# Prompt attention of a hybrid decoder layer: all heads' keys ahead of the values, four heads' scores in one row of small matmuls, four heads' outputs in another

## The chip, the cores and the metric

One core of one Trainium2 chip runs one launch of the whole layer. The metric is the device time of that launch in microseconds (us).

## The reference, cut to what matters

One layer of a decoder for a prompt (256 positions) and 8 samples of 4 positions, 288 columns in all, in float32. The change is in the prompt's half of "mixer B", an attention with three head groups of four heads; head `j` of the three groups is merged into one output with softmax weights over all three groups' keys together:

```python
z = jnp.einsum('ntd,de->nte', x, w_in)
h, gate_b, gate_c, q, k, v, g_a, g_b = jnp.split(z, _split_points(), axis=-1)
ya, conv_mix_new = _causal_dwconv(gate_c * h, conv_mix_prev, w_conv_mix)
ya = gate_b * ya
...
for g, (win, dil) in enumerate(GROUPS):          # (128,1), (512,4), (2048,16)
    o, l = _dilated_band_prompt(q[:, :, g], kg, vg, slopes[g], dil)
wg = jax.nn.softmax(jnp.stack(lses), axis=0)
yb = jnp.einsum('gnth,gnthd->nthd', wg, jnp.stack(outs)).reshape(n, t, ATT_OUT).astype(x.dtype)
mixed = jax.nn.sigmoid(g_a) * (ya @ w_branch_a) + jax.nn.sigmoid(g_b) * (yb @ w_branch_b)
x1 = _layernorm(ALPHA * x + mixed @ w_out, ln1_g, ln1_b)
```

Then a convolutional feed-forward (`w_up`, `w_down`) and a second layer norm. `yb` is needed only by the product with `w_branch_b`.

## The kernel before, in words

**Products.** TensorE (PE) multiplies 128 output features at a time. One block of weights (128 x 2048 values, 1 MB) is loaded by SP into one of three buffers `wst`, and split into a high and a low part: ACT casts `whi` (line 260), DVE subtracts `wlo` (line 260), each in two halves of the block, into four half-block buffers each. `product` (line 234) takes a block that is ready, has the next one prepared, and issues 48 matmuls (`mms`, lines 254 to 256: 16 slices of the contraction, three terms each) into one of five PSUM tiles `acc`. These five tiles are handed out in turn. A half-block's buffer comes free when PE has passed the half-block four halves earlier, so ACT's cast waits for PE, and all that stands behind the cast on ACT waits with it. The engines run their instructions in order; a scheduler sets the order when the program is built, and `behind` and `in_a_row` add edges to it.

**Order of the products.** Three query blocks (`first_three`), nine more, then for each head `j` six products: the keys and values of the three groups by turns (lines 857 to 883), then 16 triples for the short convolution (h, gate c, gate b; lines 928 to 945), the gates and the two branch products, `w_out`, the feed-forward.

**The prompt's attention** is driven by a generator, `prompt`, that `prompt_step` (line 225) advances after each product by the number that it yielded. Its pieces are:
- *Scores*: `score_row` (line 471) issues 24 small matmuls for a head (32 output columns each, line 490) behind the last matmul of a product, in one unbroken row on PE.
- *Softmax*: `softmax` (line 506): DVE adds distances (line 512), maximum (519), scale (520), ACT exponentiates (521), DVE normalises (522, 523).
- *Turning*: `weights` and `values` transpose 32 x 32 squares on DVE (line 455, helper `squares`), and `moved` puts each of 16 squares of a tile in its place: the 4 on the diagonal on POOL (line 459) at once, the other 12 as copies on ACT (463) or DVE (461), queued in `soon` and issued a few per product.
- *Outputs*: `output_row` (line 430) issues 48 small matmuls for a head (line 443) into one `acc` tile; ACT and DVE then split it into `ybh`, `ybl` (line 260), two pieces a head on each.

There are three rows of small matmuls. The first holds the scores of heads 0 to 2, behind head 2's last product. The second holds the scores of head 3 and the outputs of heads 0 to 2, behind head 3's last product. The third (`last_output`, line 704) holds head 3's output; it is issued some 27 products later from the list of the samples' steps.

**The samples' attention** runs beside it as another generator, `steps`, one step a product (paused for `N_PAUSE` = 5 products after the first score row). In a step half a tile of cached keys is multiplied, by POOL (line 613, one `tensor_tensor` of 128 x 1024) or ACT (line 611, eight activations), and DVE folds it (line 619).

**Buffers.** Keys and values of two heads stand in `kv`; the turned weights and values of heads 0 to 2 in `p_three`, `v_three`, those of head 3 in `late_p`, `late_v`.

Of the kernel before, what the change touches and what calls it, by code (L numbers as in the profile page):

```python
# [10 lines left out]
F32 = mybir.dt.float32  # L11
# [6 lines left out]
P = 128  # L18
D = 2048
KD = D // P  # L20
SEQ = 256
# [88 lines left out]
def layer_kernel(ctx: ExitStack, tc: tile.TileContext, ins, outs):  # L110
# [63 lines left out]
    def weight_list():  # L174
        for b in range(3, NB_QKV + 3 * KD):
            yield ins["w_in"][b], KD
# [176 lines left out]
    def pa_take(n):  # L353
        pa_at[0] += n
        return pa[:, pa_at[0] - n : pa_at[0]]


    m_near = [pa_take((1 + h) * P) for h in range(2)]
    m_all = [pa_take((NG - 1) * (1 + h) * P).rearrange("p (g k) -> p g k", g=NG - 1) for h in range(2)]
    k_third = [m_all[1].rearrange("p g k -> p (g k)")[:, g * SEQ : (g + 1) * SEQ] for g in range(NG - 1)]  # L360
    k_first = pa_take(SEQ)
# [9 lines left out]
    sT, s_squares = (xs_flat[:, n + c * MB * P : n + (c + 1) * MB * P].rearrange("p (b q) -> p b q", q=P) for c in range(2))  # L371


    def in_q(at, n):
        return xs_flat[:, at : at + n * P].rearrange("p (b k) -> p b k", k=P)

    p_three = sT, in_q(0, MB), in_q(MB * P, MB)
    v_three = (*v_two, in_q(2 * MB * P, 2 + NC))
# [44 lines left out]
    o_next = []  # L423
# [6 lines left out]
    def output_row():  # L430

        row = []
        quadrants = [slice(a, a + 32) for a in range(0, P, 32)]
        for j, v, p in o_next:
# [15 lines left out]
        o_next.clear()  # L450
        return row
# [19 lines left out]
    def score_row(heads):  # L471
# [5 lines left out]
        for n, (j, kT, k_class) in enumerate(heads):  # L477
            second = sb(ps, [P, 512], *(("att", F32, 2), ("long", F32, 1), ("acc",))[n])
            near_at = second[:, 3 * P :] if n == 2 else first[:, n * w : n * w + P]
            far_at = first[:, n * w : (n + 1) * w - P] if n == 2 else first[:, n * w + P : (n + 1) * w]  # L480
# [13 lines left out]
        if o_next:  # L494
            some_moves(len(soon))
            row += output_row()
# [42 lines left out]
    def early_head(j, vT):  # L539
        values(vT)  # L540
        moved(v_three[j], v_squares)
        yield 1

    def three_heads(heads, vT):

        no_keys()
        s3 = score_row(heads)
        pause[0] = N_PAUSE
        n_moves[0] = N_MOVES_TWO
        for n, j in enumerate((2, 0, 1)):  # L550
            softmax(j, s3[j])
            yield 1
            weights(p_three[j])
            no_keys()
            if n == 0:
                values(vT)
                moved(v_three[2], v_squares, True)
            yield 1
        o_next.extend(zip(range(3), v_three, p_three))

    def last_head(head, vT):

        s3 = score_row([head])
        softmax(head[0], s3[0])
        values(vT)
        moved(late_v, v_squares)
        yield 1
        weights(late_p)
        yield 2
        o_next.append((head[0], late_v, late_p))  # L570
# [3 lines left out]
    kv = dd_all[:, : 2 * 2 * NG * T].rearrange("p (b c g t) -> p b c g t", b=2, c=2, g=NG)  # L574
    sw = [dd_all[:, 2 * 2 * NG * T :], sb(wk, [P, (NB + 1) * NH * NS], "sw", bufs=1)]

    late_p, late_v = (
        dd_all[:, a * P : b * P].rearrange("p (b k) -> p b k", k=P) for a, b in ((0, MB), (MB, MB + 2 + NC))
    )
# [59 lines left out]
    def sample_steps():  # L639
# [64 lines left out]
        def last_output():  # L704
            some_moves(len(soon))
            all_heads[0] = True
            row = output_row()
            in_a_row([last_mm[0]] + row)

# [90 lines left out]
        for which, order in (("ck", far + near), ("cv", near + far)):  # L800
# [8 lines left out]
            if which == "ck":  # L809
                at(when + 2, key_spread, 1)  # L810
                at(when + 2, key_spread, 0)
                for d, what in ((3, key_sum), (3, last_output), (5, scores)):
                    at(when + d, what)
# [44 lines left out]
    for j in range(NH):  # L858
        kT, vT = (kv[:, j % 2, c] for c in range(2))
        k_class = []  # L860
        for g in range(NG):
            for t in (kT, vT):
                o = product(x).rearrange("p h a -> p a h")
                act.copy(t[:, g, :].rearrange("p (a h) -> p a h", h=2), o)
                if j == g == 0 and t is kT:
                    act.copy(k_first.rearrange("p (a h) -> p a h", h=2), o[:, :P])
                if g and t is kT:
                    if j == 2:
                        k = k_third[g - 1]
                    else:  # L870
                        k = sb(wk, [P, YW], "cy", bufs=2) if j else sb(wk, [P, UW + 2], "u", bufs=2)
                    k_class.append(k[:, :SEQ].rearrange("p (c i) -> p c i", c=NC))
                    act.copy(k_class[-1], o.rearrange("p a h -> p (a h)")[:, :SEQ].rearrange("p (i c) -> p c i", c=NC))
        pool.tensor_copy(k_s[:, :, j, :], kT[:, :, SEQ:])
        pool.tensor_copy(v_s[:, j], vT[:, :, SEQ:])
        act.dma_start(outs["o_k"][j].rearrange("p (g t) -> p g t", g=NG), kT)
        act.dma_start(outs["o_v"][j].rearrange("p (g t) -> p g t", g=NG), vT)
        heads.append((j, k_first if j == 0 else kT[:, 0], k_class))
        if j < 2:
            prompt[:] = [early_head(j, vT), 0]  # L880
        else:
            prompt[:] = [three_heads(heads[:3], vT) if j == 2 else last_head(heads[3], vT), 0]
        prompt_step()
# [605 lines left out]
```

## Time and profile before

| | |
|---|---|
| median of 3 runs | 1703.39 us (1703.29 to 1703.5) |
| profiled execution | 1703.31 us, its span 1701.1 us |
| PE busy | 1694.8 us (100%) |
| DVE, ACT, POOL busy | 1207.7 (71%), 945.5 (56%), 400.0 us (24%) |
| the three rows of small matmuls begin at | 182.33, 220.95 and 384.33 us |

The span is the time from the first to the last instruction of one profiled execution; that execution took 2.21 us more in all. In a timeline each row gives start, duration, engine, line, operation, what it writes and reads, how many instructions are merged, and in brackets how long the engine stood idle before it and what ended that. Matmuls overlap, so the distance between starts says more of PE than a duration does.

### The profile page before, as it was taken

The numbers are of one execution on the slowest core, as the hardware profiler recorded it, in microseconds if no ns is written. First come the engines' busy times: TensorE is split into PE (matmuls) and PEld (weight loads), VectorE is DVE, ScalarE is ACT, GpSimd is POOL, SyncE is SP. The second block draws the span as 40 slices with busy tenths as digits, with TensorE's granted clock in tenths as the row PEclk, the third lists the DMA queues.
The fourth block names the chain that finished last, engine by engine and source line by source line (L and its number), as shares of the span: only waits on it lengthen the run. The fifth ranks groups of instructions, "written<-read, shape, count | busy, mean of one in ns | idle before, by whom it ended". The sixth has DMA issues, their size and how long they took to land.

```text
span 1701.1 us, 34294 instructions
## 1 busy us (share of the span) xinstructions
PE 1694.8 (100%) x14086; PEld 1690.4 (99%) x14086; DVE 1207.7 (71%) x1574; ACT 945.5 (56%) x1696; POOL 400.0 (24%) x530
## 2 busy tenths in 40 slices
PE   9999999999999999999999999999999999999998
PEld 9999999999999999999999999999999999999998
DVE  5476779889887777655888888855686554555575
ACT  5577686665666655544556565544455443344454
POOL 0122243223332221110464233300111100011165
PEclk9999999999999999999999999999999999999999
DMA  8788778666678888677766666666666666666663
GB/s 293 294 300 348 283 283 317 239 253 243 249 297 314 332 306 337 210 259 257 284 230 223 225 252 235 230 223 226 235 228 252 224 233 236 249 224 230 226 241 137
DMA packets 59805, 436.17 MB, mean 256 GB/s; under 512 B 7744, under 2 KB 12608, under 8 KB 19904
## 3 DMA queue, kind: packets, MB, share of 16 engines
q1 hardware_dynamic: 58352, 430.15, 68.7%
q10 hardware_dynamic: 1296, 3.83, 0.6%
q8 instruction: 110, 1.80, 0.4%
q14 instruction: 47, 0.39, 0.1%
HBM read 427.50 MB, written 94.53 MB: 307 GB/s over the span
## 4 chain that ended last, share of the span: by engine, by line
PE 99%; POOL 0%; ACT 0%; POOLq 0%; issue 0%; ACTq 0%
PE acc L254 32%; PE acc L255 32%; PE acc L256 32%; PE acc L339 1%; POOL sw L1145 0%; PE acc L443 0%; PE acc L270 0%; PE att L490 0%; PE acc L490 0%; POOLq L1484 0%; PE long L490 0%; ACT yah L1187 0%; PE att L1043 0%; ACT cache L1103 0%; PE att L1039 0%
## 5 line engine op out<-in xcount | busy, mean ns | idle before, releaser
L260 DVE TENSOR_TENSOR wlo<-wst,whi 128x1024 fp32r<-128x1024 f32 (+1 forms) x578 | 743.8, 1289 | 391.0 <-ACT whi L260 388.3
L260 ACT CAST whi<-wst 128x1024 fp32r<-128x1024 f32 (+1 forms) x578 | 588.9, 1021 | 652.7 <-PE acc L255 593.0
L254 PE MATMUL acc<-xh,whi 128*128 128x288 f32 (+1 forms) x3216 | 920.6, 286 | 0.0
L256 PE MATMUL acc<-xh,wlo 128*128 128x288 f32 (+1 forms) x3216 | 920.4, 286 | 0.0
L255 PE MATMUL acc<-xl,whi 128*128 128x288 f32 (+1 forms) x3216 | 920.3, 286 | 0.0
L254 PEld LDWEIGHTS acc<-xh,whi 128*128 128x128 f32 x3216 | 607.8, 189 | 0.5 <-issue 0.4
L256 PEld LDWEIGHTS acc<-xh,wlo 128*128 128x128 f32 x3216 | 607.8, 189 | 0.0
L255 PEld LDWEIGHTS acc<-xl,whi 128*128 128x128 f32 x3216 | 607.8, 189 | 0.0
L255 PE MATMUL acc<-yal,whi 128*128 128x288 f32 x1216 | 347.7, 286 | 0.0
L256 PE MATMUL acc<-yah,wlo 128*128 128x288 f32 x1216 | 347.7, 286 | 0.0
L254 PE MATMUL acc<-yah,whi 128*128 128x288 f32 x1216 | 347.6, 286 | 0.0
L255 PEld LDWEIGHTS acc<-yal,whi 128*128 128x128 f32 x1216 | 229.8, 189 | 0.0
L256 PEld LDWEIGHTS acc<-yah,wlo 128*128 128x128 f32 x1216 | 229.8, 189 | 0.0
L254 PEld LDWEIGHTS acc<-yah,whi 128*128 128x128 f32 x1216 | 229.8, 189 | 0.0
L909 POOL COPY qk_s<-u 128x2 f32<-128x2 f32 x44 | 36.5, 830 | 532.6 <-ACT u L1247 412.1
L897 DVE SCALAR_TENSOR_TENSOR cy<-u,prm,cy 128x304 f32<-128x304 f32 x120 | 75.8, 632 | 8.1 <-ACT cy L895 4.9
L613 POOL TENSOR_TENSOR cache<-cache,cst 128x1024 f32<-128x1024 f32 x16 | 34.5, 2160 | 110.0 <-DMA cache<-in_cv 94.9
L613 POOL TENSOR_TENSOR cache<-cache,qk_s 128x1024 f32<-128x1024 f32 x16 | 33.9, 2122 | 74.3 <-DMA cache<-in_ck 74.0
L260 ACT CAST yah<-ya 128x288 fp32r<-128x288 f32 x76 | 32.6, 429 | 32.1 <-DVE ya L920 14.5
L611 ACT ACTIVATE cache<-cache,qk_s 128x128 f32<-128x128 f32 x128 | 40.6, 392 | 0.0
L890 POOL COPY u<-prm 128x16 f32<-128x16 f32 x60 | 40.4, 674 | 0.2 <-issue 0.2
L611 ACT ACTIVATE cache<-cache,cst 128x128 f32<-128x128 f32 x128 | 40.0, 390 | 0.0
(277 smaller groups left out, 1181.3 us busy)
## 6 DMA issues: line engine op xcount, KB each, us to landing
wst<-in_w_in SPq DMA_DIRECT2D x112, 1024.0 KB, 5.5
wst<-in_w_up SPq DMA_DIRECT2D x88, 1024.0 KB, 4.9
wst<-in_w_down SPq DMA_DIRECT2D x32, 1024.0 KB, 4.9
cache<-in_ck SPq DMA_DIRECT2D x18, 1024.0 KB, 8.2
cache<-in_cv SPq DMA_DIRECT2D x18, 1024.0 KB, 8.6
wst<-in_w_a SPq DMA_DIRECT2D x16, 1024.0 KB, 6.1
wst<-in_w_out SPq DMA_DIRECT2D x16, 1024.0 KB, 5.0
wst<-in_w_down SPq DMA_DIRECT2D x16, 768.0 KB, 4.5
```

The lines of the kernel that those rows point to most:

```text
L254: pe.matmul(out, hi[:, c, :], xh_k, start=k == 0, stop=False)
L255: pe.matmul(out, hi[:, c, :], xl_k, start=False, stop=False)
L256: last_mm[0] = pe.matmul(out, lo[:, c, :], xh_k, start=False, stop=k == nk - 1)
L260: return act.copy(hi, src), dve.tensor_tensor(lo, src, f32(hi), ALU.subtract)
L339: i = pe.matmul(o[b], first_w(term == 2, b, k), xk, start=k == 0 and term == 0, stop=k == KD - 1 and term == 2,)
L611: behind(act.activation(o[:, a, b], t[:, a, b], AF.Copy, scale=w[:, a, b : b + 1]), w_split[0])
L613: behind(pool.tensor_tensor(o, t, w.unsqueeze(3).broadcast_to([P, *n]), ALU.mult), w_split[1])
L890: pool.tensor_copy(tail[:, :, 0:2], prm[:, state : state + 2 * NB].rearrange("p (b r) -> p b r", b=NB))
L897: dve.scalar_tensor_tensor(y, u[:, i : i + YW], prm[:, w0 + i : w0 + i + 1], y, ALU.mult, ALU.add)
L909: pool.tensor_copy(dst[:, 0:2], u[:, SEQ : SEQ + 2])
```

## The change

The projection's blocks are now taken in another order: all 12 key products of the four heads first, then all 12 value products. Behind the last key product one row holds the scores of all four heads (the fourth head's long scores go to a second `acc` tile). The softmaxes then run beside the value products in the order of heads 2, 3, 0, 1; each head's values are turned when they are there (heads 1 and 2 with the copies on DVE, 0 and 3 on ACT). Behind the second product of the convolution (gate c of the first triple) one row holds the outputs of all four heads. The row out of the samples' steps is gone. The three-row version's number of small matmuls is kept: 96 for scores and 192 for outputs.

```diff
     def weight_list():
-        for b in range(3, NB_QKV + 3 * KD):
-            yield ins["w_in"][b], KD
+        n = NG * NH
+        for blocks in (range(3, n), range(n, NB_QKV, 2), range(n + 1, NB_QKV, 2), range(NB_QKV, NB_QKV + 3 * KD)):
+            for b in blocks:
+                yield ins["w_in"][b], KD
...
     def output_row():
-        row = []
+        row = [last_mm[0]]
...
-        for j, v, p in o_next:
+        for j, (v, p) in enumerate(zip(v_heads, p_heads)):
...
-        o_next.clear()
-        return row
+        in_a_row(row)
...
     def score_row(heads):
-            second = sb(ps, [P, 512], *(("att", F32, 2), ("long", F32, 1), ("acc",))[n])
...
+            second = sb(ps, [P, 512], *(("att", F32, 2), ("long", F32, 1), ("acc",), ("acc",))[n])
...
-        if o_next:
-            some_moves(len(soon))
-            row += output_row()
         in_a_row(row)
         return s3
...
+    def values_of(j, on_dve=False):
+        some_moves(len(soon))
+        values(v_done[j])
+        moved(v_heads[j], v_squares, on_dve)
+
+    def four_heads(heads):
         no_keys()
         s3 = score_row(heads)
         pause[0] = N_PAUSE
         n_moves[0] = N_MOVES_TWO
-        for n, j in enumerate((2, 0, 1)):
+        for n, j in enumerate((2, 3, 0, 1)):
             softmax(j, s3[j])
             yield 1
-            weights(p_three[j])
+            weights(p_heads[j])
             no_keys()
...
+            yield 2 if n == 0 else 1
+            if n:
+                values_of(n - 1, n > 1)
+                yield 1 if n < NH - 1 else 2
+        values_of(NH - 1)
         yield 2
+        some_moves(len(soon))
+        output_row()
...
     for j in range(NH):
...
+            o = product(x).rearrange("p h a -> p a h")
+            act.copy(kv[:, j, g].rearrange("p (a h) -> p a h", h=2), o)
...
+        heads.append((j, kv[:, j, 0], k_class))
+    prompt[:] = [four_heads(heads), 0]
+    prompt_step()
+    for j in range(NH):
+        for g in range(NG):
+            o = product(x).rearrange("p h a -> p a h")
+            act.copy(kv[:, j, g].rearrange("p (a h) -> p a h", h=2), o)
...
+        v_done.append(kv[:, j])
+    prompt_step()
```

The line numbers of the changed program stand some lines off those of before (254 to 256 are 256 to 258 there, 260 is 262, 443 is 446, 455 is 457, 463 is 465, 613 is 604, 619 is 610, 936 is 920).

**PE, at the end of the row that holds the outputs.** A name like `acc_2938` is one handing-out of an `acc` tile. Before, on PE, the end of the second row (the last score matmuls went ahead of it), with what each waits for:

```order
L443 MATMUL acc_2833<-yah_88,yal_178 32x256 [waits Activation_49,Pool_49]
L443 MATMUL acc_2833<-yah_88,yal_178 32x256 x3
L443 MATMUL acc_2833<-yah_88,yal_178 32x2x32 x16
L443 MATMUL acc_2833<-yah_88,yal_178 32x128 x4
L443 MATMUL acc_2862<-yah_88 32x256 x4
L443 MATMUL acc_2862<-yah_88 32x2x32 x16
L443 MATMUL acc_2862<-yah_88 32x128 x4
L254 MATMUL acc_2938<-xh_86,whi_2702 128x288
```

And of the change, the fourth head of the one row of outputs (`acc_3076`) and the first matmul of the product behind it, gate b of the first triple (`acc_3138`):

```order
L446 MATMUL acc_3076<-yah_88,yal_178 32x256 [waits Activation_49,Pool_49]
L446 MATMUL acc_3076<-yah_88,yal_178 32x256 [waits Pool_49] x2
L446 MATMUL acc_3076<-yah_88,yal_178 32x256 [waits Activation_49,Pool_49]
L446 MATMUL acc_3076<-yah_88,yal_178 32x2x32 x16
L446 MATMUL acc_3076<-yah_88,yal_178 32x128 x4
L256 MATMUL acc_3138<-xh_86,whi_2927 128x288 [waits DVE_49,PE_49]
```

What moved: before, the product behind the row waits for no other engine; now its first matmul waits for DVE. With four output tiles in a row, the next product gets the `acc` tile of the product just ahead of the row (`acc_2937`, gate c), and that is read by DVE's line 920.

**ACT, around that row.** Before, on ACT, behind head 3's last value product (`acc_2712`):

```order
L611 ACTIVATE cache_2002<-cache_2002,qk_s_182 128x128 x2
L864 COPY dd_184<-acc_2712 128x288
L611 ACTIVATE cache_2002<-cache_2002,qk_s_182 128x128 x6
L463 COPY dd_184<-yal_178 32x6x32 x6
L877 DMA out_o_v<-dd_184 128x864
L260 CAST ybh_180<-acc_2804 128x128
L260 CAST ybh_180<-acc_2833 128x128
```

Of the change, on ACT: the 12 copies of head 3's turned values (line 465, `yal_178`) stand between the casts of the weights for the products gate b (`whi_2927`, `whi_2931`) and the next triple's h (`whi_3119`); `h_2923` is the product h of the first triple:

```order
L262 CAST whi_2927<-wst_2925 128x1024
L465 COPY yal_178<-yal_178 32x6x32 x9
L262 CAST whi_2931<-wst_2925 128x1024
L465 COPY yal_178<-yal_178 32x6x32 x2
L915 COPY h_2923<-acc_2865 128x288
L465 COPY yal_178<-yal_178 32x6x32
L262 CAST whi_3119<-wst_3116 128x1024
```

What moved: head 3's values used to be turned long after the second row and were needed at the third; now they are the last thing that the row of outputs needs, and a weight cast and the copy of h stand among their copies.

**DVE, up to the read of `acc_2937`.** Before, on DVE, ahead of and behind the second row's start:

```order
L455 STREAM_TRANSPOSE yah_88<-yal_178 128x640
L260 TENSOR_TENSOR wlo_2703<-wst_2700,whi_2702 128x1024
L260 TENSOR_TENSOR wlo_2707<-wst_2700,whi_2706 128x1024
L619 TENSOR_REDUCE dd_184<-cache_1862 128x2x4x4
L455 STREAM_TRANSPOSE yal_178<-dd_184 128x256
L455 STREAM_TRANSPOSE yal_178<-dd_184 128x4x64
L260 TENSOR_TENSOR wlo_2920<-wst_2917,whi_2919 128x1024
```

Of the change, from the copies of head 2's values on DVE (line 463) to gate c's read (line 920):

```order
L463 COPY yah_88<-yal_178 32x6x32 x12
L262 TENSOR_TENSOR wlo_2847<-wst_2844,whi_2846 128x1024
L457 STREAM_TRANSPOSE yal_178<-dd_184 128x4x64
L262 TENSOR_TENSOR wlo_2851<-wst_2844,whi_2850 128x1024
L610 TENSOR_REDUCE dd_184<-cache_2508 128x2x4x4
L457 STREAM_TRANSPOSE yal_178<-dd_184 128x256
L457 STREAM_TRANSPOSE yal_178<-dd_184 128x4x64
L262 TENSOR_TENSOR wlo_2928<-wst_2925,whi_2927 128x1024
L262 TENSOR_TENSOR wlo_2932<-wst_2925,whi_2931 128x1024
L610 TENSOR_REDUCE dd_184<-cache_2508 128x2x4x4
L262 TENSOR_TENSOR wlo_3120<-wst_3116,whi_3119 128x1024
L920 TENSOR_TENSOR u_3105<-h_2923,acc_2937 128x2x128
```

What moved: the transposes of head 3's values (line 457) stand behind those twelve copies, and the read that frees `acc_2937` stands behind the split of the block for the product after next (`wlo_3120`), which needs ACT's cast `whi_3119`.

More of the change, by code (lines that the diff above doesn't have):

```diff
@@ L421, in turned @@
             yield
-    o_next = []
     def far_keys(h, g):
@@ L537, in weights @@
         moved(p, s_squares)
[L539 to L544, printed above, removed]
+    v_done = []
+    def values_of(j, on_dve=False):
[3 more added lines that the diff above has]
+    def four_heads(heads):
         no_keys()
@@ L702, in new_spread @@
             )
[L704 to L708, printed above, removed]
         def by_fours(blocks):
@@ L811, in sample_steps @@
                 at(when + 2, key_spread, 0)
-                for d, what in ((3, key_sum), (3, last_output), (5, scores)):
+                for d, what in ((3, key_sum), (5, scores)):
                     at(when + d, what)
@@ L858, in layer_kernel @@
     for j in range(NH):
-        kT, vT = (kv[:, j % 2, c] for c in range(2))
         k_class = []
         for g in range(NG):
[L862 to L882, printed above, removed]
```

45 lines of the change are left out of this document (21 added, 24 removed).

## The prediction

> **What bounds the kernel now.** I read the page's busy times first, then PE's waits, then the page's groups.
>
> ```profile
> PE 1694.8 (100%) x14086; PEld 1690.4 (99%) x14086; DVE 1207.7 (71%) x1574; ACT 945.5 (56%) x1696; POOL 400.0 (24%) x530
> ...
> L260 DVE TENSOR_TENSOR wlo<-wst,whi 128x1024 fp32r<-128x1024 f32 (+1 forms) x578 | 743.8, 1289 | 391.0 <-ACT whi L260 388.3
> L260 ACT CAST whi<-wst 128x1024 fp32r<-128x1024 f32 (+1 forms) x578 | 588.9, 1021 | 652.7 <-PE acc L255 593.0
> ```
>
> ```profile
> PE acc L270 <- PEq L1476: 0.8, 1, 0.8
> PE acc L1134 <- DVE yah L1139: 0.3, 2, 0.2
> ```
>
> PE is busy throughout, and its list of waits has only these two rows, 1.1 us in all, at the start and in the tail. So no transfer, split or eviction is late anywhere now. ACT's casts wait 593 us for PE to free a weight buffer: ACT and DVE run ahead and are held by PE. The change can gain only by taking time from PE, and can lose without limit by making PE wait.
>
> **The rows of small matmuls, read from PE's timeline**: the last product's matmul before each row, the first behind it, and the one after that.
>
> ```profile
> 182.12 0.29 PE L256 MATMUL acc<-xh,wlo 128*128 128x288 f32 x1
> ...
> 185.47 0.39 PE L254 MATMUL acc<-xh,whi 128*128 128x288 f32 x1
> ...
> 220.73 0.29 PE L256 MATMUL acc<-xh,wlo 128*128 128x288 f32 x1
> ...
> 225.38 0.39 PE L254 MATMUL acc<-xh,whi 128*128 128x288 f32 x1
> 225.60 0.29 PE L255 MATMUL acc<-xl,whi 128*128 128x288 f32 x1
> ...
> 384.12 0.29 PE L256 MATMUL acc<-xh,wlo 128*128 128x288 f32 x1
> ...
> 385.57 0.39 PE L254 MATMUL acc<-xh,whi 128*128 128x288 f32 x1
> 385.79 0.29 PE L255 MATMUL acc<-xl,whi 128*128 128x288 f32 x1
> ```
>
> From 225.60 to 384.12 stand 27 products less one matmul, 1294 steps, so a matmul takes 0.1225 us and a product of 48 takes 5.88. The three rows take 3.35 us (three heads' scores), 4.65 (one head's scores, three outputs) and 1.45 (one output). With s for a head's scores, o for its output and e for entering and leaving a row, 3s+e = 3.35, s+3o+e = 4.65 and o+e = 1.45 give s = 1.00, o = 1.10, e = 0.35.
>
> **Step 1, one row fewer.** The 96 and 192 small matmuls stay. The new rows take 4 x 1.00 + 0.35 = 4.35 and 4 x 1.10 + 0.35 = 4.75, together 9.10 instead of 9.45. Where the third row goes, an ordinary step of 0.12 is left, and the second step behind a row (385.57 to 385.79, 0.22 instead of 0.12) goes too: **0.33 us less on PE**. If nothing waits, that is the whole effect.
>
> **Step 2, the key products first.** As many products, blocks and evictions as before; moved evictions and their output DMAs lie beside PE. The score row now follows head 3's last key product itself, so that product's two copies on ACT are new on its path. They stand behind at most two casts (0.95 us each, row 208.20 below); with 0.3 and 0.4 for themselves they end some 2.6 us after the product; head 3's scores come 3.0 us into the row, and its third group later still. I take 0; without that cover it is 2.6.
>
> **Step 3, softmaxes and values beside twelve value products.** Before, three softmaxes lay in six products while the samples' steps paused. Now four softmaxes and four turnings lie in fourteen products, and the steps go on after the fifth. Here I made a ledger by hand: the order of the changed program on ACT and DVE, with spacings from starts in the timeline of before. First DVE, a stretch without idle time but the 0.4 us at 207.7:
>
> ```profile
> 198.25 0.22 DVE L522 RECIPROCAL st<-st 128x1 f32<-128x1 f32 x2
> 198.44 0.68 DVE L523 TENSOR_SCALAR yal<-yal,st 128x256 f32<-128x256 f32 x2
> 199.15 1.23 DVE L260 TENSOR_TENSOR wlo<-wst,whi 128x1024 fp32r<-128x1024 f32 x1
> 200.41 3.17 DVE L461 COPY yah<-yal 32x192 f32<-32x192 f32 x12
> 203.61 0.85 DVE L455 STREAM_TRANSPOSE yah<-yal 128x640 f32<-128x640 f32 x1
> 204.38 1.18 DVE L260 TENSOR_TENSOR wlo<-wst,whi 128x1024 fp32r<-128x1024 f32 x1
> 205.48 0.47 DVE L512 SCALAR_TENSOR_TENSOR yal<-yal,att 128x128 f32<-128x128 f32 x3
> 205.88 0.67 DVE L512 SCALAR_TENSOR_TENSOR yal<-yal,long 128x256 f32<-128x256 f32 x3
> 206.47 1.21 DVE L260 TENSOR_TENSOR wlo<-wst,whi 128x1024 fp32r<-128x1024 f32 x1
> 208.11 0.88 DVE L519 TENSOR_REDUCE st<-yal 128x1 f32<-128x256 f32 x2 [0.43 <-POOL yal L504]
> 208.91 0.27 DVE L520 TENSOR_SCALAR st<-st 128x1 f32<-128x1 f32 x2
> ...
> 150.18 1.24 DVE L619 TRANSPOSE_TENSOR_REDUCE dd<-cache 128x32 f32<-128x1024 f32 x1
> 151.34 0.61 DVE L455 STREAM_TRANSPOSE yal<-dd 128x256 f32<-128x256 f32 x1
> ...
> 184.54 1.52 DVE L455 STREAM_TRANSPOSE yal<-dd 128x256 f32<-128x256 f32 x3
> ...
> 240.03 0.52 DVE L936 TENSOR_TENSOR u<-h,acc 128x256 f32<-128x256 f32 x2
> ```
>
> Then ACT: an eviction, moves of a turned tile (of weights, then of values), a cast, two exponentials, six scalings of cached keys.
>
> ```profile
> 205.16 0.40 ACT L864 COPY dd<-acc 128x288 f32<-128x288 f32 x1
> 205.46 0.38 ACT L873 COPY cy<-acc 128x256 f32<-128x256 f32 x1
> 205.85 2.33 ACT L463 COPY yah<-yah 32x160 f32<-32x160 f32 x7
> 208.20 1.04 ACT L260 CAST whi<-wst 128x1024 fp32r<-128x1024 f32 x1
> 209.15 0.51 ACT L521 ACTIVATE yal<-yal,st 128x256 f32<-128x256 f32 x1
> ...
> 210.25 1.03 ACT L260 CAST whi<-wst 128x1024 fp32r<-128x1024 f32 x1
> ...
> 152.92 1.43 ACT L463 COPY yal<-yal 32x192 f32<-32x192 f32 x4
> ...
> 156.21 1.86 ACT L611 ACTIVATE cache<-cache,qk_s 128x128 f32<-128x128 f32 x6
> ```
>
> Time zero is the first value product's start; the value products are V1 to V12, those of the convolution C1 (h), C2 (gate c), C3 (gate b).
> - **a, ACT bound.** PE frees V4's last half-block at 23.6, so ACT's cast of V6's second half ends at 24.7. Behind it stand twelve moves of weights (0.33 each, 4.0), an eviction (0.4), two exponentials (1.1), five casts (4.8), 16 scalings and two evictions (5.5) and twelve moves of values (4.3): 20.1 us, to 44.8, when the cast for V9 is done.
> - **b, DVE bound.** Six splits (1.15 each, 6.9), three folds (1.16, 3.5), adding (1.0), maxima and scales (1.1), normalising (0.9), one set of value transposes (1.5), twelve moves (3.2), the transpose of weights (0.8): 18.9, to 63.7. On the way V11's and V12's first low halves are done at about 59.0 and 64.8; PE wants them at 59.05 and 64.9.
> - **c, ACT, then DVE.** Twelve moves and a cast, 5.0, to 68.7. Then DVE: four splits (4.6), two folds (2.3), twelve moves (3.2), three transposes (1.5): 11.6, to 80.3.
> - **d, the new wait.** Head 3's values are now turned, so ACT, from 79.8, does twelve moves (4.3), two casts (2.1) and the copy of h (0.4), to 86.6. DVE does the split for C4 (1.15) and the product of gate c (0.5), which frees the fifth `acc` tile: 88.25.
>
> PE is ready for C3 at 14 x 5.88 + 0.1 + 4.63 = 87.05 (0.1 for the longer second step behind the score row; 4.63 is the output row's 4.75 less the ordinary step in it). So **PE waits 1.2 us** at C3. Queued behind that DVE product are the split for C4's second half and the output's eight `ybl`; C4 needs them only 5.9 us later, and they take about 4, so nothing further waits. The price of this wait has no row: it lies between 0 (the ledger too long by 1.2 of 65 us, 2%) and the collisions below.
>
> **Step 4, collisions of DVE with POOL.** The ledger's spacings are free of them; the trace isn't:
>
> ```profile
> 245.93 1.89 POOL L613 TENSOR_TENSOR cache<-cache,qk_s 128x1024 f32<-128x1024 f32 x1
> ...
> 246.28 2.63 DVE L260 TENSOR_TENSOR wlo<-wst,whi 128x1024 fp32r<-128x1024 f32 x1
> ```
>
> ```profile
> L260 DVE TENSOR_TENSOR wlo<-wst,whi 128x1024 fp32r<-128x1024 f32 x55 | 76.7, 1398 | 27.7 <-ACT whi L260 27.5
> ```
>
> A split that starts inside POOL's multiply takes 2.63 instead of 1.2 us: it ends 1.1 us after POOL's end. The last row groups the 55 splits between 130 and 300 us: their mean is 1.40 against 1.23 undisturbed (199.15), so 0.17 a split; the ten splits in b and c make 1.7. Bounds: 0, if both of POOL's multiplies there miss, and 3.8, if each holds DVE for its full 1.9. I take 1.6, near the mean, and DVE has no idle time there to swallow it.
>
> [...]
>
> [...]
>
> **Sum**, against the profiled execution's 1703.31: -0.33 + 1.2 + 1.6 = +2.5, 1705.8. The median of before stands 0.08 above that execution, which changes nothing.
>
> **Rivals.**
> - *All hidden.* The ledger is 65 us of DVE and ACT work end to end, and it is 2 to 4% too long or the collisions miss. For it: no wait of PE shows anywhere now. Against it: DVE has no idle row in b and c. Then 1703.31 - 0.33 = 1703.0, faster by 0.02%, which no verdict can tell.
> - *Both collisions at full price* (the slower side). POOL's multiplies of two cached tiles stand right behind the diagonal moves of heads 1 and 2, so each begins about 1.6 us after a set of transposes, where DVE has splits and then twelve moves. If those moves are held as the splits are, both cost 1.9: 1703.31 - 0.33 + 1.2 + 3.8 = 1708.0. It decides from 2.6 us of collisions on, where the sum passes 1706.8.
> - *The score row waits for the last key* (step 2): 2.6 us at once, which gives ACT and DVE the same room; 1703.31 - 0.33 + 2.6 = 1705.6 if nothing else waits. The row's order, head 3 last, speaks against it.
>
> **How the numbers follow.** A difference of 0.2% (3.4 us) is about what a measurement of this kernel can tell from no change, so the bounds are 1700.0 and 1706.8. Chances: forecast (1704.4 to 1706.8) 0.45; all hidden (1702.9 to 1704.4) 0.27; collisions at full price (1706.8 to 1709) 0.22; the score row 0.04, within 0.2%; the rest 0.02, half of it slower, half faster. That gives faster 0.01, same 0.76, slower 0.23. The range leaves out the last part of the collisions and the rest: 1702.9 to 1708.2.
>
> **What would show it.** In the changed profile: two rows of 4.35 and 4.75 us and none near 384 (step 1); PE's waits with a row of `acc` for DVE's line 920, about 1 to 3 us at the product behind the outputs (3d); if collisions bite, PE waiting for `wlo` at V11 or V12 and splits above 2 us near POOL's multiplies (4). It is wrong if PE's list of waits stays as it is, or if PE waits outside the fourteen products.

## The result, and the profile after

The changed kernel takes 1708.26 us in the median of 8 runs (1706.58 to 1709.23), the kernel before beside it 1703.47 (1703.17 to 1704.05): a ratio of 1.0027, interval 1.0016 to 1.0038. It is slower by 0.27%, more than the 0.2% that the prediction takes for about the least that can be told. The time lies at the upper end of the predicted range: 0.06 us above its 1708.2, while the difference, 4.79 us, is just inside the 4.89 that the range allows over 1703.31. It also varies more: 2.65 us from the lowest to the highest run against 0.88.

The profiled execution of the changed kernel took 1709.18 us, its span is 1707.4; the time outside the span is 1.8 us, where it was 2.2. The lines of its page that answer to those shown of before:

```profile
PE 1695.0 (99%) x14086; PEld 1690.0 (99%) x14086; DVE 1211.8 (71%) x1586; ACT 939.9 (55%) x1683; POOL 395.4 (23%) x531
...
L262 DVE TENSOR_TENSOR wlo<-wst,whi 128x1024 fp32r<-128x1024 f32 (+1 forms) x578 | 740.3, 1283 | 389.4 <-ACT whi L262 387.0
L262 ACT CAST whi<-wst 128x1024 fp32r<-128x1024 f32 (+1 forms) x578 | 588.1, 1021 | 654.2 <-PE acc L257 595.1
```

PE's busy time is as before (1695.0 against 1694.8), so the 6.25 us that the span grew are time in which PE stands. PE's list of waits (us in all, times, longest) had two rows before:

```profile
PE acc L257 <- issue: 1.9, 1, 1.9
PE acc L256 <- DVE u L920: 1.4, 1, 1.4
PE acc L258 <- DVE wlo L262: 1.1, 2, 0.8
PE acc L272 <- PEq L1460: 0.8, 1, 0.8
PE acc L341 <- ACT yal L308: 0.7, 1, 0.7
PE acc L1118 <- DVE yah L1123: 0.3, 2, 0.2
```

The second and third row are waits of the kind the prediction spoke of; the fourth and the last stood there before, and the fifth lies at the start. The first is new and of another kind: "issue" means that the profile shows nothing that PE waited for. PE's timeline shows where each stands:

```profile
147.22 0.29 PE L258 MATMUL acc<-xh,wlo 128*128 128x288 f32 x1
147.44 0.32 PE L493 MATMUL att<-dd,yah 128*32 128x128 f32 x4
...
151.58 0.39 PE L256 MATMUL acc<-xh,whi 128*128 128x288 f32 x1
...
153.15 0.29 PE L256 MATMUL acc<-xh,whi 128*128 128x288 f32 x1
155.33 0.39 PE L257 MATMUL acc<-xl,whi 128*128 128x288 f32 x1 [1.90 <-issue]
...
212.77 0.29 PE L257 MATMUL acc<-xl,whi 128*128 128x288 f32 x1
213.37 0.39 PE L258 MATMUL acc<-xh,wlo 128*128 128x288 f32 x1 [0.31 <-DVE wlo L262]
...
232.08 0.39 PE L258 MATMUL acc<-xh,wlo 128*128 128x288 f32 x1 [0.81 <-DVE wlo L262]
...
237.70 0.29 PE L258 MATMUL acc<-xh,wlo 128*128 128x288 f32 x1
...
243.94 0.36 PE L256 MATMUL acc<-xh,whi 128*128 128x288 f32 x1 [1.44 <-DVE u L920]
```

The score row goes from 147.22 to 151.58, 4.36 us; the output row, entered at 237.70, takes 4.74 without the wait behind it (4.35 and 4.75 were forecast). Behind V1's 13th matmul PE stands from 153.15 to 155.33, 2.18 instead of 0.12. The next low halves late are those of V11 (0.60 from 212.77 to 213.37) and C2 (1.09); C3 starts 1.71 us after the last output matmul starts. Less an ordinary step each (0.12, and 0.20 at the end of the output row, as in the profile of pause13 below, where nothing waits), that is 2.06, 0.48, 0.97 and 1.51 us. (The trace holds two records for each small matmul of the program: 96 of the program and 192 records in either row. The 192 that the sections above name for the outputs are these records.)

Reading the times of PE's 1168th matmul (the last ahead of the score row here), of its 8001st and of its last in both traces divides the 6.25 us:

| stretch | before | after | difference |
|---|---|---|---|
| start to the 1168th matmul | 146.84 | 147.22 | +0.38 |
| to the 8001st (all rows lie here) | 799.64 | 804.61 | +4.97 |
| to the last | 749.27 | 749.28 | +0.01 |
| last matmul to the end of the span | 5.37 | 6.27 | +0.90 |

The 4.97 are 5.02 of the four stops, some 0.3 for the long step behind a stop, and 0.33 less for the row that is gone. The 0.38 lies at the start, to which the list's row for line 341 belongs: the 1168th matmul starts between 146.8 and 147.5 us in the profiles of nearly all variants below that leave the start alone (149.0 in one, pool_out). The prediction had nothing for the 2.06 of the first stop or the 0.90 at the end. So there are three questions: what makes the three DVE waits, what is the "issue", and what lengthens the tail.

### The profile page after: what moved, and what is told of

Same layout as the page of the kernel before. It is cut to its first block, busy times and chain, and to the rows that moved or that the text cites. A ratio compares the mean times of both kernels' runs of the same rounds, so it can differ in the third digit from the quotient of the medians.

```text
span 1707.4 us, 34293 instructions
## 1 busy us (share of the span) xinstructions
PE 1695.0 (99%) x14086; PEld 1690.0 (99%) x14086; DVE 1211.8 (71%) x1586; ACT 939.9 (55%) x1683; POOL 395.4 (23%) x531
## 4 chain that ended last, share of the span: by engine, by line
PE 94%; ACT 2%; DVE 2%; issue 1%; POOL 0%; DMA 0%; SPq 0%; POOLq 0%; ACTq 0%; DVEq 0%
PE acc L256 31%; PE acc L257 31%; PE acc L258 31%; PE acc L341 1%; ACT whi L262 0%; ACT yal L465 0%; ACT yah L465 0%; DVE dd L610 0%; DVE wlo L262 0%; POOL sw L1129 0%; DMA yah<-in_x 0%; ACT cache L602 0%; DVE yah L463 0%; DVE yal L463 0%; DVE yal L457 0%
## 5 line engine op out<-in xcount | busy, mean ns | idle before, releaser
L610 DVE TRANSPOSE_TENSOR_REDUCE sw<-cache 128x32 f32<-128x1024 f32 x32 | 39.4, 1236 | 0.0
```

The costliest lines, as they stand in the source:

```text
L610: behind(dve.tensor_reduce(out, t.rearrange("p (a b q c) -> p a b q c", a=out.shape[1], b=out.shape[2], c=32), AX.X, ALU.add, apply_transp ...
```

## The experiments

Three theories, named in the expectations: **CHAIN** (the three waits come from the DVE and ACT work beside the value products, as in steps 3 and 4), **FETCH** (the stop in V1 is PE out of instructions) and **TAIL** (instruction packets lengthen the end). What speaks for FETCH in the trace of after is one row of the DMA queues, here between 152.8 and 153.9 us:

```profile
q8 instruction: 1, 0.02, 5.3%
```

Over the whole span this queue brings 110 packets of 16,384 bytes, one for about 128 weight loads and 128 matmuls: PE's instructions. In the median one comes 15.7 us after the other, as long as 128 ordinary matmuls take. The row's 192 small ones take 4.1 us.

**The changed kernel again** (nothing edited), for a second profile, and later five rounds of it.

> The changed kernel once more, for a second profile. Two theories for the 4.8 us that it is slower. CHAIN: the DVE and ACT work beside the value products ends late, so PE waits for the low half at the eleventh value product and at gate c, and for line 920 at gate b; in the first profile these were 0.5 + 1.0 + 1.5 = 3.0 us. FETCH: the 2.1 us that PE stands in the first value product, put down to 'issue', is PE out of instructions. CHAIN expects the three waits again within 0.5 us each. FETCH expects a stall behind the score row again, at the same matmul, but of another length (0 to 3 us), since it depends on when a 16 KB instruction packet gets through among the weight loads. If the stall is a fixed dependence of the program instead (RIVAL), it has the same 2.1 us.

> The changed kernel unchanged, beside the others on one chip. FETCH and CHAIN both say that its time varies: the stall in the first value product between 0 and 2.1 us, and the wait at the eleventh value product 0.5 us where a copy of DVE is held by POOL's multiply, 1.7 us where a split is. So runs between 1705.5 and 1709.5 us, a median of about 1707.8, against a spread of 1 us for the kernel before.

Measured: 1707.82 us in the single run of the first; 1707.90 (1707.18 to 1710.99, 10 runs) in the second, a ratio of 1.0026 (1.0017 to 1.0036). The DVE waits repeat to 0.02 us: 0.48, 0.97 and 1.52 in both profiles. The stop in V1 is at the same matmul, PE's 1373rd, and lasts 0.84 and 1.14 us instead of 2.06. So it isn't a wait of fixed length; whether it hangs on the count of matmuls is tried next.

**More matmuls ahead: shift112 and shift40** (the diff is that of shift112; shift40 has 12 and 44).

```
-N_WARM = 16
+N_WARM = 6
+N_SMALL = 122
...
+    for _ in range(N_SMALL):
+        pe.matmul(o[:32, :32], zeros[0][:, :32], zeros[0][:, :32], start=True, stop=True)
```

> The changed kernel with 6 wide and 122 tiny matmuls as warm-up instead of 16 wide ones: about as long, but 112 matmuls more ahead of everything, so that the borders of PE's 16 KB instruction packets (about 128 matmuls) fall elsewhere: in the score row behind about 93 of its 192 records instead of 77, and then 221 instead of 205. From one border to the next PE then takes some 6 us on both sides of the row instead of 4.2. FETCH expects the stall in the first value product at 0 to 0.6 us instead of 2.1, and about 1706.5 us in all. RIVAL (a fixed dependence) expects the stall of 2.1 us where it was, and 1708.3. CHAIN expects its three waits, 3.0 us in all, in either case.

> The changed kernel with 12 wide and 44 tiny matmuls as warm-up: 40 matmuls more ahead of everything, so that a border of PE's instruction packets falls at about record 37 of the score row's 192 and the next at 165, both inside the row. From border to border PE then takes only some 2.6 us. In the three profiles with a stall PE went on 2.4 us after the packet's start. FETCH therefore expects a stall again, this time inside the score row, of 0.6 us if the packet starts at once and up to 4 us if it starts as late as before (3.9 us behind the border), and none behind the row. RIVAL expects the stall, if any, at the same matmul of the first value product as before. The start takes about 0.8 us longer, so the time is 1708 to 1711 us.

shift112 has no stop behind the row: PE's list of waits has no "issue", and from the last matmul ahead of the row it takes 9.36 us to the 41st of V1, as without any stop. In shift40 the stop is inside the row. Its list of waits and its timeline:

```profile
PE att L496 <- issue: 2.9, 1, 2.9
```

```profile
151.68 0.23 PE L496 MATMUL att<-yah 128*32 128x32 f32 x5
154.77 0.27 PE L496 MATMUL att<-yah 128*32 128x32 f32 x2 [2.86 <-issue]
```

It again stands behind PE's 1373rd matmul, which is now a score matmul, not one of V1. The same count in another place of the program is what FETCH says and RIVAL can't. The times miss what was expected: 1711.78 us (1711.19 to 1712.12, 5 runs; ratio 1.0046, 1.0034 to 1.0059) and 1712.68 (1711.63 to 1715.19, 4 runs; ratio 1.0055, 1.0041 to 1.0068). The first product starts at 8.87 us in shift112, not 4.9, since a tiny warm-up matmul takes longer than I had reckoned (some 0.05 us, an estimate: 8.87 less the 0.8 ahead of the first and six wide ones at the 0.24 of after, over 122); that is the 4 us. In shift40 the start is later too, the wait at V11 is 1.69 us, and one more low half came late near the start. The largest part of what its profiled execution (1715.19 us) took more is another: from 154.1 us, near the end of the stop of 3 us, to 160.9 the granted clock is 0.50, and ordinary matmuls start 0.24 us apart instead of 0.12:

```profile
157.66 0.45 PE L259 MATMUL acc<-xh,wlo 128*128 128x288 f32 x1
157.90 0.45 PE L257 MATMUL acc<-xh,whi 128*128 128x288 f32 x1
```

From the last matmul ahead of the row to the 41st of V1 it takes 15.41 us instead of 9.36: 3.04 for the stop and 3.01 for the slow matmuls. Behind the 2.06 us of after, the clock stays at 1.00.

**What delays the packet: quiet and load_later.** One takes the store of head 3's keys away from the row, the other the load of a cached tile.

```
 quiet:
-        act.dma_start(outs["o_k"][j].rearrange("p (g t) -> p g t", g=NG), kv[:, j])
+        if j < NH - 1:
+            act.dma_start(outs["o_k"][j].rearrange("p (g t) -> p g t", g=NG), kv[:, j])
...
+            if j == 0 and g == 1:
+                act.dma_start(outs["o_k"][NH - 1].rearrange("p (g t) -> p g t", g=NG), kv[:, NH - 1])
```

```
 load_later:
-                        at(when - LATER, load, which, n)
+                        at(when - LATER + 1, load, which, n)
```

> The changed kernel, in which the store of head 3's keys (432 KB on ACT's queue) is issued two products later, so that fewer packets are on their way while PE is in the score row. If PE's late instruction packet is late because it queues behind the transfers there (the DMA engines are busy 0.99 of the time between 147 and 153 us), it starts earlier than in the changed kernel (151.6 to 152.9 us there, a start at 150.9 or earlier gives no stall) and the stall in the first value product falls to 0.5 us or less: about 1 us less. If its lateness has another cause, the stall stays between 0.8 and 2.1 us. The three waits of CHAIN stay, 3.0 us, or 4.2 where the split and not a copy is held at the first collision.

> The changed kernel with the loads of the cached tiles one step later. The load of 1 MB that SP issues at 145.1 us, 2.3 us ahead of the score row, then falls away from there (it comes ahead of the last key products or behind the pause), so that beside the row only the store of head 3's keys and the weight load issued at 149.7 are on their way. If PE's instruction packet starts late because it queues behind transfers, the DMA engines' share between 147 and 152 us falls below 0.8 (0.94 to 0.98 in the changed kernel), the packet starts at 150.6 us or earlier, and no stall is left behind the row: 1 to 1.3 us less than the changed kernel beside the others (1707.9), so 1706.7. If its lateness has another cause, it starts between 151.5 and 152.9 as in the changed kernel, with a stall of 0.8 to 2.1 us. The waits of CHAIN stay about 3 us in either case.

quiet takes 1707.20 us (1706.74 to 1709.52, 11 runs; ratio 1.0022, 1.0014 to 1.0031). Its stop is 0.88 us, within what the unedited kernel shows and not the 0.5 or less that was hoped for, and the DMA engines are as busy as in the changed kernel (1.02 of the time from 147 to 152 us, against 0.98): that store alone isn't it. load_later did what was expected. The windows from 147 to 152 us (engines' busy times, clock, DMA share, GB/s), first of after, then of load_later, then load_later's list of waits:

```profile
147.00:152.00 5.00, 5.00 (x200) 4.08 (x199) 2.46 (x8) 1.62 (x3) 1.43 (x5) 1.00 0.98 353
```

```profile
147.00:152.00 5.00, 5.00 (x199) 4.17 (x199) 2.85 (x9) 1.62 (x3) 1.44 (x5) 1.00 0.65 221
```

```profile
PE acc L256 <- DVE u L920: 1.5, 1, 1.5
PE acc L258 <- DVE wlo L262: 1.1, 2, 0.8
PE acc L272 <- PEq L1460: 0.8, 1, 0.8
PE acc L1118 <- DVE yah L1123: 0.3, 2, 0.2
PE acc L341 <- ACT yal L308: 0.2, 1, 0.2
```

The share falls from 0.98 to 0.65, the packet starts at 149.33 and the row "issue" is gone from the list; the three DVE waits are as they were. Its time is 1706.75 us (1706.14 to 1708.10, 11 runs; ratio 1.0018, 1.0009 to 1.0027), 1.1 below again5, as expected, though the two intervals overlap. All profiles in which the row starts at the same matmul, times counted from the row's start (PE wants its 1374th matmul at 5.83):

| profile | packet starts | PE goes on | stop |
|---|---|---|---|
| after | 5.45 | 7.89 | 2.06 |
| again5 | 4.66 | 6.97 | 1.14 |
| tail_after | 4.65 | 7.02 | 1.18 |
| again | 4.27 | 6.67 | 0.84 |
| quiet | 3.94 | 6.71 | 0.88 |
| tile_att | 3.30 | 5.98 | 0.14 |
| pool_out | 3.26 | | none |
| best | 2.88 | | none |
| pause13 | 2.32 | | none |
| load_later | 2.28 | | none |

PE goes on 2.3 to 2.8 us after the packet's start (in shift40 2.2; the packet itself takes 0.9 to 1.4), and where the packet starts by 3.26 there is no stop. This settles FETCH. That transfers under way delay the packet is borne out at the extremes: shares of 0.65 (load_later) and of 0.87 to 0.88 (best, pause13) go with starts at 2.3 to 2.9, shares of 0.94 to 1.02 with 3.3 to 5.5. Among the latter the share doesn't order the starts, so what sets the length of the delay there stays open.

How far ahead of its use a packet comes is read by counting PE's matmuls up to each packet's start. Counting from 0, packet n starts, in 109 of the 110 cases of after, when PE is 72 to 117 matmuls beyond the 128n-th (median 86); in the kernel before 108 of the 110 lie 74 to 130 beyond, and the two others, 203 and 171, start right behind its first two rows, at 186.86 and 226.80 us. The one exception of after is the late packet, the tenth: it starts at 152.88 us, 218 beyond, at PE's 1370th matmul. By the other 109, an estimate, it was due between the 1224th and the 1269th, inside the row, which holds the 1169th to the 1360th; in the kernel before, the packet of the same number starts at the 1235th. The packet ahead of it starts at 141.91 us, at PE's 1124th matmul, and PE runs out of instructions behind the 1373rd, 249 matmuls and as many weight loads later. The other engines' packets in this trace have 8,192 bytes.

**The fifth acc tile: tile_att.** Head 0's output goes into a score tile that is free by then, so C3 takes an older `acc` tile.

```
-            po = sb(ps, [P, SEQ], "acc")
+            po = sb(ps, [P, 512], "att", F32, 2)[:, :SEQ] if j == 0 else sb(ps, [P, SEQ], "acc")
```

> The changed kernel with the first head's output in one of the two score tiles (att), which are free by then, instead of in an acc tile. So gate b takes the acc tile of the product h, read long before, and not that of gate c, which line 920 must read. CHAIN as the prediction put it (gate b waits for the fifth acc tile) expects PE's wait for line 920 gone, 1.4 to 1.7 us less, the other two waits as they were: about 1706.8 us. The rival, that the late DVE work only shows up one product later (the next low halves, or the eviction), expects a new wait of PE of 1 us or more at gate b or behind it, and 1708 us.

Measured: 1706.19 us (1705.35 to 1708.71, 11 runs), a ratio of 1.0017 (1.0008 to 1.0026). Its list of waits:

```profile
PE acc L258 <- DVE wlo L262: 1.1, 2, 0.8
PE acc L272 <- PEq L1460: 0.8, 1, 0.8
PE acc L341 <- ACT xh L313: 0.7, 1, 0.7
PE acc L1118 <- DVE yah L1123: 0.3, 2, 0.2
```

The row for line 920 is gone and no other took its place; V11 and C2 wait as before. Step 3d is confirmed: the wait is for the tile. (The stop in V1 is 0.14 us in this profile, so not all that the time gained is the tile's.)

**POOL's multiplies left out: pool_out.**

```
-        behind(pool.tensor_tensor(o, t, w.unsqueeze(3).broadcast_to([P, *n]), ALU.mult), w_split[1])
+        if prompt[0] is None:
+            behind(pool.tensor_tensor(o, t, w.unsqueeze(3).broadcast_to([P, *n]), ALU.mult), w_split[1])
```

> The changed kernel without POOL's multiplies of cached tiles from the score row to the output row (four of them; the samples' outputs are not the reference's for that). In the changed kernel two of them hold the first of DVE's copies of turned values, 0.45 and 0.86 us. CHAIN with collisions expects PE's waits at the eleventh value product and at gate c down from 1.45 us in all to 0.2 or less, and the wait at gate b from 1.5 to about 1.0: some 1.9 us less, 1706.4 us. If the waits come from the load of DVE and ACT alone, they stay at 3 us, and the time at 1708.3.

Left out are the five multiplies that start from 182.27 to 237.88 us in the trace of after; the expectation counts four. Measured: 1706.69 us (1705.90 to 1707.82, 11 runs), a ratio of 1.0017 (1.0008 to 1.0026). Its list of waits:

```profile
PE acc L256 <- DVE u L921: 1.4, 1, 1.4
PE acc L272 <- PEq L1461: 0.8, 1, 0.8
PE acc L341 <- ACT xh L313: 0.6, 1, 0.6
PE acc L1119 <- DVE yah L1124: 0.3, 2, 0.2
```

Both `wlo` waits are gone, so they were collisions with POOL. The time doesn't price them by itself, since this profile has no stop in V1 either and a tail of 6.72 us. The wait at C3 didn't fall, against my expectation: without the collisions PE arrives there earlier by about as much as DVE (1.4 us each, counted from the score row and without the stop in V1). In the trace of after the collisions stand here:

```profile
206.87 2.75 POOL L604 TENSOR_TENSOR cache<-cache,qk_s 128x1024 f32<-128x1024 f32 x1
...
209.03 0.70 DVE L463 COPY yal<-yal 32x192 f32<-32x192 f32 x1
...
225.82 1.90 POOL L604 TENSOR_TENSOR cache<-cache,qk_s 128x1024 f32<-128x1024 f32 x1
...
226.72 1.38 DVE L463 COPY yah<-yal 32x192 f32<-32x192 f32 x2
```

The copy at 209.03 starts inside POOL's multiply and ends 0.11 us after it: 0.70 instead of 0.25. The first of the two at 226.72 takes 1.11 (1.38 less the second's 0.25 and a gap). Two copies of DVE lose 0.45 and 0.86 us. POOL's first multiply started inside a split and took 2.75 instead of 1.90. In tail_after the phase was a fraction of a us different and a split paid:

```profile
204.94 2.75 POOL L607 TENSOR_TENSOR cache<-cache,qk_s 128x1024 f32<-128x1024 f32 x1
...
205.98 2.79 DVE L262 TENSOR_TENSOR wlo<-wst,whi 128x1024 fp32r<-128x1024 f32 x1
```

There V11 waits 1.69 us instead of 0.48.

**The samples' steps kept away: pause13.**

```
-N_PAUSE = 5
+N_PAUSE = 13
-PACE = 12, 13
+PACE = 11, 13
```

> The changed kernel with the samples' steps paused for 13 products behind the score row instead of 5, and packed a little closer elsewhere (11 instead of 12 of 13 half tiles' spacing), so that they are done by the same time. Beside the value products DVE then has no folds, ACT no scalings and POOL no multiplies. CHAIN expects the waits at the eleventh value product, gate c and gate b gone (3.0 us less), the stall behind the score row still there: about 1705.3 us, or 1703.3 if that stall doesn't show in this one. If the softmaxes and turnings alone are too much for the fourteen products, the waits stay above 1.5 us in all.

With this spacing one partial sum of the samples is added a step before the last fold that belongs in it, so the samples' outputs aren't the reference's; the instructions are as many. Measured: 1703.29 us (1702.91 to 1704.16, 11 runs), a ratio of 0.9997 (0.9989 to 1.0006). Its list of waits is that of the kernel before:

```profile
PE acc L272 <- PEq L1460: 0.8, 1, 0.8
PE acc L1118 <- DVE yah L1123: 0.3, 2, 0.2
```

The softmaxes and turnings alone fit into the fourteen products. From the 1168th to the 8001st matmul PE takes 799.31 us, against 799.64 before: 0.33 less, step 1's figure. The packet came in time too (2.32), as the pause also moved the cached tiles' loads; so this experiment doesn't separate CHAIN from FETCH, the others do.

**The tail: tail_after and tail_before.** In the trace of after, from 1702 to 1707 us, two packets of other engines' instructions arrive while the last output is stored:

```profile
q14 instruction: 2, 0.02, 0.8%
```

The edit of tail_after (tail_before has 10 and 0, in the kernel before):

```
+    for e, n in ((dve, 24), (pool, 16)):
+        for _ in range(n):
+            e.memset(sb(wk, [P, 4], "st", bufs=4)[:, 0:1], 0.0)
```

> The changed kernel with 24 one-column memsets on DVE and 16 on POOL at the start, where both wait for the input. They shift the borders of these two engines' 8 KB instruction packets. In the changed kernel two such packets arrive 2.4 and 3.3 us behind PE's last matmul, beside the last output DMA, and from that matmul to the end of the span it takes 6.27 us; before, no packet arrives there and it takes 5.37. TAIL theory (the packets delay the last DMA) expects 5.4 us and no packet there, 0.9 us less: about 1707.4 us. Rival (the tail is longer because the ends of the output lie otherwise) expects 6.27 us still, 1708.3.

> The kernel before with 10 one-column memsets on DVE at the start, so that DVE runs as many instructions as in the changed kernel and its stream passes the last border just at the end. TAIL theory expects a packet beside the last output DMA and 0.4 to 0.9 us from it: 5.8 to 6.3 us from PE's last matmul to the end, 1704.3 to 1704.7 us in all. Rival expects no change, 5.37 us and 1703.8.

tail_after has no such packet there and 5.32 us from PE's last matmul to the end, instead of 6.27. It takes 1706.77 us (1705.92 to 1708.97, 11 runs; ratio 1.0020, 1.0012 to 1.0029), where 1707.4 was expected. In tail_before one packet arrives, from 1697.5 to 1702.5 us, and the tail grows from 5.37 to 6.29:

```profile
q14 instruction: 1, 0.01, 0.4%
```

The issues of the last stores say the same (KB each, us from issue to landing), first in the window of tail_after, then in that of tail_before:

```profile
out_o_y<-yah SPq DMA_DIRECT2D x2, 144.0 KB, 2.5
```

```profile
out_o_y<-yah SPq DMA_DIRECT2D x2, 144.0 KB, 3.5
```

They took 3.4 in after and 2.5 before. So both profiles bear TAIL out, in both directions. The times of tail_before alone don't: 1704.02 us (1703.80 to 1705.88, 11 runs) against 1703.60, a ratio of 1.0004 (0.9996 to 1.0013). Its spans are 0.8 us longer than those of before beside it (medians 1702.2 and 1701.4), but the time outside the span is 0.35 shorter (1.79 against 2.14), as it is in every variant here; why isn't known. TAIL isn't all that lengthens an end either: pause13's tail is 5.86 us with its last stores landing as before, since one of POOL's closing instructions starts late (5.22 us behind PE's last matmul, 4.87 before).

**All of it together: best.** pause13 with the memsets of tail_after, and the partial sum put behind its fold.

```
-                at(when - 2 * NB * PACE[0] // PACE[1], of_all, 1)
+                at(when + 1 - 2 * NB * PACE[0] // PACE[1], of_all, 1)
```

> The changed kernel with the pause of 13 products, the samples' steps packed closer, the summing step of the samples put one step later so that it stays behind the last fold, and the 24 and 16 one-column memsets that move the borders of DVE's and POOL's instruction packets away from the end. CHAIN, FETCH and TAIL together expect no wait at the eleventh value product, gate c and gate b, no stall behind the score row if the packet starts by 150.9 us, and 5.3 to 5.4 us from PE's last matmul to the end. PE then has one row less, 0.33 us: 1703.3 us, 0.3 less than the kernel before, a difference at the edge of what can be told. If something of the three is wrong, it is 1704.5 or more.

Measured: 1702.95 us (1702.55 to 1704.55, 11 runs) against 1703.58, a ratio of 0.9996 (0.9987 to 1.0004). Its list of waits:

```profile
PE acc L275 <- PEq L1463: 0.8, 1, 0.8
PE acc L344 <- ACT xh L316: 0.7, 1, 0.7
PE acc L1121 <- DVE yah L1126: 0.3, 2, 0.2
```

Nothing of the loss is left: 799.31 us again for the stretch with the rows, 5.33 for the tail. Against the kernel before it is a gain of 0.04% that the interval can't tell from none, and 0.35 of its 0.63 us lie outside the span.

## Where the prediction was right and where it was wrong, point by point

- **Step 1** was right in its figure and wrong in its reach. The row that is gone is worth 0.33 us (pause13, best). The failing step is its silent premise that a longer row costs only its matmuls: a row of 192 instead of 144 score records, at another place among PE's instruction packets, can use up its instructions before the next packet is there. The sum had no term for it; it is 0.84 to 2.06 us in the three profiles of the changed kernel, and none where the packet comes early.
- **Step 2** held: the score row starts 0.22 us after the last key product's matmul, without a wait. Two rivals fall with that and with the waits seen: the score row waiting for its last key, and all hidden.
- **Step 3d** was right in mechanism, place and nearly in size: 1.51 us for the forecast 1.2, and tile_att shows the tile as the cause. The ledger held within 2 us over 90: counted from V1 and its stop, V11's first low half was 0.7 later than forecast, and line 920 ended 1.9 later.
- **Step 4** had the right size on the wrong operations: 0.48 + 0.97 = 1.45 us for the forecast 1.6 (2.66 in tail_after), at V11 and C2, where V11 or V12 was named, and not on top of the wait at C3. I put it on splits; in most profiles copies of turned values were held. That is the mechanism of the rival on both collisions, whose 1.9 each no run shows: it was 0.45 and 0.86, since the multiplies were partly over when the copies started. That copies can be held is what 0.70 and 1.11 us instead of 0.25 show. The trace of before has a row on it that I had not read: four copies of one size on DVE, beside four `tensor_tensor` of POOL, that took 216, 438 and 494 ns (shortest, median, longest):

```profile
L637 DVE COPY sw<-qk_s x4: 216/438/494, 694.4 to 695.6; 32x128 f32<-32x128 f32 x4
...
694.49 2.00 POOL L631 TENSOR_TENSOR sw<-qk_s 32x128 f32<-32x128 f32 x4 [27.14 <-DVE qk_s L758]
```

- **The tail** wasn't in the prediction. By what was read here the 0.90 us there come from where DVE's and POOL's instruction streams happen to end; tail_before, where DVE's count alone moved, brought one of the two packets, and that the other is POOL's is inferred.

Together: 1703.3 - 0.33 + 1.51 + 1.45 = 1705.9, the forecast almost. With some 1 us of FETCH, 0.9 of TAIL, 0.3 for the steps behind the stops and 0.35 less outside the span it is 1707.8; 1707.90 (again5) and 1708.26 were measured. The upper part of the range and the chance for slower by over 0.2% stood on collisions at full price; that the time came out at the upper end of the range is luck, since what brought it there was something else.

## What to carry to other kernels

When small instructions are gathered into longer rows on an engine that never waits, ask how fast it uses up instructions (here 192 records in 4.1 us, where 128 ordinary matmuls take 15.7) and what transfers are under way at that time, not only how long the row takes. A wait called "issue" of varying length, always at the same count of instructions (here 0.84 to 2.06 us, behind the 1373rd matmul), is read best beside the instruction packets in the DMA queues, and is tried by moving the count. Where the gain sought is as small as a row's edge (0.33 us), the ends of the instruction streams alone can move the span by more (0.9 us).

## What the runs showed of the hardware that was not expected

- PE stops when a 16,384-byte instruction packet is late: it goes on 2.2 to 2.8 us after the packet's start, always behind the same count of matmuls (the 1373rd, in two different places of the program).
- A stop can cost twice: with the 3 us of shift40 the granted clock fell to 0.50 for 6.8 us, and the matmuls behind the stop took 3.0 us more; with stops of up to 2.06 us it stayed at 1.00.
- An instruction packet of 8,192 bytes that arrives while the last output is stored goes with a longer end: 0.9 us where one starts 3.3 us behind PE's last matmul (tail_before, and after, with a second at 2.4), 0.5 where the only one starts at 2.4 (load_later, 5.88 us in all). The last stores then land up to 1 us later (3.4 and 3.5 us from issue instead of 2.5).
- In the collisions read here between POOL and DVE the one that started second paid: POOL's multiply 2.75 instead of 1.90 us, a copy 0.70 or 1.11 instead of 0.25, a split 2.79 instead of 1.23. A fraction of a us of phase decides which, and so whether PE waits 0.5 or 1.7 us.
